# Making every fourth lo weight piece by an adding transfer in a one-core decoder trunk

## The chip, the cores and the metric

The kernel runs on one core of a Trainium2 chip. Time is device microseconds of that core. Its engines are TensorE (PE, with its weight loads as PEld), VectorE (DVE), ScalarE (ACT), GpSimd (POOL) and SyncE (SP). SP and GpSimd each issue transfers from a queue of their own; all transfers run on the core's 16 DMA engines.

## The reference

Two layers of a decoder trunk over 256 rows of width 2048, all in fp32. Layer 0 mixes by a convolution module and by differential attention, layer 1 by a gated short convolution; each layer then cross-attends into 256 memory rows and applies a squared-ReLU MLP with 8192 hidden columns:

```python
def reference(x, mem, ...):
    mem_n = rms_norm(mem, mem_norm_g)
    for l in range(DEPTH):
        hn = rms_norm(x, mix_norm_g[l])
        if l % 2 == 0:
            x = x + even_mixer(hn, ...)      # convolution module and differential attention
        else:
            x = x + odd_mixer(hn, ...)       # gated short convolution
        x = x + cross_attention(rms_norm(x, xattn_norm_g[l]), mem_n, xq_w[l], xk_w[l], xv_w[l], xo_w[l])
        x = x + sq_relu_mlp(rms_norm(x, mlp_norm_g[l]), mlp_w1[l], mlp_w2[l])
    return rms_norm(x, final_norm_g)
```

Nearly all of the work is products with weights: 1008 pieces of 128 x 1024 fp32 values, 512 KB each, every one read once.

## The kernel before, in words

A product in near-fp32 precision is made of three products in the shorter type fp32r. Weights and activations are each split into a half `hi`, the value rounded to fp32r, and a half `lo`, what the rounding lost; hi x hi, hi x lo and lo x hi are summed.

The function `weights` (L150) delivers one piece. It takes a tile `raw` and two tiles `whi` and `wlo` from rings of buffers, and gives three instructions: SP loads the piece from HBM into `raw` (L162), ScalarE copies it rounded into `whi` (L163), and VectorE writes `wlo = raw - whi` (L164). `calls` counts the pieces. The ring of `raw` has five buffers (shared with sixteen loads of the memory rows, `memraw`), those of `whi` and `wlo` three each. A buffer is taken again only when its last reader is done: `raw` when both copies of it are made, `whi` and `wlo` when TensorE's matmuls with them are.

Most products go through `wide_piece`: eight matmuls with hi weights against activations hi and lo side by side (512 columns), and eight with lo weights against the hi activations (256 columns). In the second piece of a projection one hi matmul stands behind the lo ones, so that TensorE's order is 8 hi, 8 lo, 7 hi, 8 lo, 1 hi. `proj_rows` (tiles `mmr`) and the narrow `proj` (keys, gates) use the same pieces.

Instructions run in order on each engine, and loads are issued in order by SP. Buffers decide how far the engines run ahead of TensorE, and a scheduler places the instructions of different pieces, residuals, norms and attention among one another. The token "lo" fixes the order of the subtractions among VectorE's work. Beside the weights, VectorE does residuals, the 31-tap convolution and the lo halves of activations; ScalarE does hi halves, squares, exponentials and evacuations of PSUM (`sum`, L208); GpSimd, after the start, only clears `ahl` eight times (L435) in the attention of layer 0.

Small tiles come from the pool `tmp`: `t32` (seven buffers), `rb` (three), `pexp` (four) and `diag` (two). `diag` is the diagonal matrix by which `spread` lays a norm's row values over the partitions with a matmul `nmb`.

Of the kernel before, what the change touches and what calls it, by code (L numbers as in the profile page):

```python
# [10 lines left out]
F32 = mybir.dt.float32  # L11
F32R = mybir.dt.float32r
I32 = mybir.dt.int32
AF = mybir.ActivationFunctionType
ALU = mybir.AluOpType
AX = mybir.AxisListType

P = 128
D = 2048
S = 256  # L20
# [25 lines left out]
def trunk(ctx: ExitStack, tc: tile.TileContext, d):  # L46
    nc = tc.nc
    V, A, T, G = nc.vector, nc.scalar, nc.tensor, nc.gpsimd
# [1 line left out]
    const = ctx.enter_context(tc.tile_pool(name="const", bufs=1))  # L50
    xpool = ctx.enter_context(tc.tile_pool(name="xpool", bufs=1))
    half = ctx.enter_context(tc.tile_pool(name="half", bufs=13))
    wraw = ctx.enter_context(tc.tile_pool(name="wraw", bufs=5))
    wspl = ctx.enter_context(tc.tile_pool(name="wspl", bufs=3))
    prob = ctx.enter_context(tc.tile_pool(name="prob", bufs=4))
    tmp = ctx.enter_context(tc.tile_pool(name="tmp", bufs=2))
    small = ctx.enter_context(tc.tile_pool(name="small", bufs=4))
# [4 lines left out]
    def f(ap):  # L62
        return ap.bitcast(F32)
# [23 lines left out]
    def col(name, c=0):  # L87
        i = VEC[name] + c
        return gvec[:, i:i + 1] if i < NG else vec[:, i - NG:i - NG + 1]
# [5 lines left out]
    def load_vec():  # L95
        nc.sync.dma_start(out=vec, in_=d["vec"][:, NG:])
        lv = vec[:, VEC["lam"] - NG:VEC["lam"] - NG + 256].rearrange("p (a b) -> p a b", a=4)
        lp = tmp.tile([P, S], F32, tag="t32", name="lp", bufs=7)[:, :128].rearrange("p (a b) -> p a b", a=2)
        V.tensor_tensor(lp, lv[:, 0:4:2], lv[:, 1:4:2], op=ALU.mult)
        ls = small.tile([P, 2], F32, name="ls", bufs=1)  # L100
        V.reduce_sum(out=ls, in_=lp, axis=AX.X)
        le = small.tile([P, 2], F32, name="le", bufs=1)
        A.activation(le, ls, AF.Exp)
        V.tensor_tensor(neglam, le[:, 1:2], le[:, 0:1], op=ALU.subtract)
        V.tensor_scalar(neglam, neglam, -LAM0, None, op0=ALU.add)
        V.tensor_scalar(subg, col("subln_g"), 1.0 - LAM0, None, op0=ALU.mult)
# [10 lines left out]
    rate, calls, strict = [0], [0], [False]  # L117

    def ordered(i, token):

        tc.stamp_issue_order_token(i.ins, token)
# [7 lines left out]
    def run_later(n, upto):  # L129
        while n and background and background[0][0] <= upto:  # L130
            background.pop(0)[1]()
            n -= 1

    def run_stages(upto):
        while True:
            due = [e for e in stages if e[0] <= upto]
            if not due:
                return
            stages.remove(due[0])
            due[0][1]()  # L140

    def mm(*a, **k):
        i = T.matmul(*a, **k)  # L143
        if strict[0]:
            ordered(i, "pe")
# [6 lines left out]
    def weights(src):  # L152
        run_later(rate[0], calls[0])
        run_stages(calls[0])
        calls[0] += 1
        raw = wraw.tile([P, 1024], F32, tag="raw", name="raw")
        hi = wspl.tile([P, 1024], F32R, tag="whi", name="whi")
        lo = wspl.tile([P, 1024], F32R, tag="wlo", name="wlo")
        n = 512 if calls[0] == 1 else 1024
        for i in range(0, 1024, n):  # L160
            o = slice(i, i + n)
            nc.sync.dma_start(out=raw[:, o], in_=src[:, o])  # L162
            A.copy(hi[:, o], raw[:, o])  # L163
            ordered(V.tensor_tensor(lo[:, o], raw[:, o], f(hi[:, o]), op=ALU.subtract), "lo")  # L164
        return hi, lo

    def block(ps, hi, lo, act, k, first, last):
# [16 lines left out]
    def proj_group(srcs, act, order=(0, 1), wide=True):  # L184


        pp = [ps_mm.tile([P, 512], F32, tag="mm", name="mm")[:, :(2 * S if wide else S)] for _ in srcs]
        for g in order:
            if g == order[-1] and len(srcs) > 1:
                run_stages(END)  # L190
            for src, ps in zip(srcs, pp):
                hi, lo = weights(src[:, g * 1024:(g + 1) * 1024])
                first, last = g == order[0], g == order[-1]
                if wide:
                    wide_piece(ps, hi, lo, act, g * 8, first, last)
                    continue
                for j in range(8):
                    w = slice(j * P, (j + 1) * P)
                    block(ps, hi[:, w], lo[:, w], act, g * 8 + j, first and j == 0, last and j == 7)
        return pp  # L200
# [4 lines left out]
    def summed(ps):  # L205

        t = tmp32("sum")
        A.copy(t, ps[:, S:])  # L208
        V.tensor_tensor(t, ps[:, :S], t, op=ALU.add)  # L209
        return t  # L210
# [58 lines left out]
    def spread(rows):  # L269
        ps = ps_nm.tile([P, 512], F32, tag="nm", name="nmb")[:, :S]  # L270
        for t in range(2):
            dg = tmp.tile([P, P], F32, tag="diag", name="diag")
            A.activation(dg, ident, AF.Copy, scale=rows[:, t:t + 1])
            mm(ps[:, t * P:(t + 1) * P], ones, dg, start=True, stop=True)
        return ps

    def rstd_rows(acc, n, pool=None, name="rrow"):

        v = small.tile([P, 2], F32, tag="rs_v", name="rs_v")
        V.tensor_scalar(v, mean_rows(acc, n), EPS, None, op0=ALU.add)  # L280
        return rsqrt(v, 2, pool, name)
# [12 lines left out]
        return y  # L294

    def to_sbuf(ps, pool=None, name="rb"):
        r = pool.tile([P, S], F32, tag=name, name=name) if pool else tmp.tile([P, S], F32, tag="rb", name=name, bufs=3)
        A.copy(r, ps)
        return r

    def rstd(acc, n):
        return to_sbuf(spread(rstd_rows(acc, n)))
# [13 lines left out]
            V.tensor_tensor(self.acc, self.acc, sq, op=ALU.add)  # L316

    def tmp32(name="t32"):
        return tmp.tile([P, S], F32, tag="t32", name=name, bufs=7)

    def residual(k, ps, nxt, ss, gname):

# [15 lines left out]
        return softmax_from(src, nm, width, scale)  # L338

    def softmax_from(src, bias, width, scale):  # L340
        p = tmp.tile([P, S], F32, tag="pexp", name="pexp", bufs=4)
        sm = small.tile([P, 1], F32, tag="psum", name="psum")
        A.activation(p[:, :width], src, AF.Exp, bias=bias, scale=scale, accum_out=sm)
        inv = small.tile([P, 1], F32, tag="pinv", name="pinv")
        V.reciprocal(inv, sm)
        return p, inv
# [4 lines left out]
    def even_mixer():  # L351
# [17 lines left out]
        def x_spread():  # L369
            rr["bc"] = to_sbuf(spread(rr["col"]))  # L370
# [4 lines left out]
        strict[0] = True  # L375
        pps = [proj_rows(d["even_v"][0], xa.hi, xa.lo, load_x)]
        load_vec()
        pps.append(proj_rows(d["even_v"][1], xa.hi, xa.lo))
        rc, r = rr["col"], rr["bc"]
# [19 lines left out]
        def scores(h, q, k):  # L399
            pr = {}  # L400
            banks = [ps_at.tile([P, 512], F32, tag="at", name="sc") for _ in range(2)]
            for t in range(2):
                tq = slice(t * P, (t + 1) * P)
                for c in range(2):
                    e = slice(c * 64, (c + 1) * 64)
                    ps = banks[c][:, t * S:(t + 1) * S]
                    mm(ps, q[e, 0, tq], k[e, 0], start=True, stop=False)
                    mm(ps, q[e, 1, tq], k[e, 0], start=False, stop=False)
                    mm(ps, q[e, 0, tq], k[e, 1], start=False, stop=True)
            for t in range(2):  # L410
                wd = (t + 1) * P
                for c in range(2):
                    sc = tmp32("scm")
                    mn = small.tile([P, 1], F32, tag="mx", name="mn")
                    V.tensor_tensor_reduce(
                        out=sc[:, :wd], in0=banks[c][:, t * S:t * S + wd],
                        in1=mask.rearrange("p a b -> p (a b)")[:, S - wd:],
                        scale=1.0, scalar=-NEG, op0=ALU.add, op1=ALU.min, accum_out=mn)
                    pr[t, c] = softmax_from(sc[:, :wd], mn, wd, -1.0)
            for t in range(2):  # L420
                wd = (t + 1) * P
                (p0, i0), (p1, i1) = pr[t, 0], pr[t, 1]
                V.tensor_tensor(i1, i1, neglam, op=ALU.mult)
                A.activation(p1[:, :wd], p1[:, :wd], AF.Copy, scale=i1)
                V.scalar_tensor_tensor(p0[:, :wd], p0[:, :wd], i0, p1[:, :wd], op0=ALU.mult, op1=ALU.add)
            stage(D1, lambda: turn(h, pr))
# [38 lines left out]
        def head_norm(h, orow):  # L465
            on = tmp32("on")
            V.tensor_tensor(on, orig[:, h], to_sbuf(spread(orow[:, 2 * h:2 * h + 2])), op=ALU.mult)
            rr["co"].put(h, on)
# [269 lines left out]
    r = spread(rstd_rows(ss.acc, D))  # L738
    for g in range(8):
        o = slice(2 * g, 2 * g + 2)  # L740
# [62 lines left out]
```

## Time and profile before

| what | value |
|---|---|
| median of 3 runs | 2928.85 us (2928.50 to 2928.92) |
| the profiled execution's own time | 2928.61 us |
| its span, first to last instruction | 2926.8 us |
| granted TensorE clock | 0.998 |
| TensorE busy | 2907.2 us, 99% |
| VectorE busy | 2000.0 us, 68% |
| ScalarE busy | 1456.8 us, 50% |
| GpSimd busy | 3.9 us |
| transfers | 540.12 MB; SP's queue 58.0% of 16 engines' span |

The span is the stretch that the profiler saw; the time has 1.8 us around it. A group of instructions is named by its line, engine, and the tiles it writes and reads (`wlo<-raw,whi`). Idle time of an engine that ends with "<-" was ended by the one named. TensorE's busy time covers pipelined matmuls, so 99% says that it seldom waited, not that it ran at its peak.

### The profile page before, as it was taken

The page shows a single profiled execution, that of the slowest core. Times are in us where ns is not written, and L with a number is a line of the kernel's source. Part 1 is how long each engine was busy: PE and PEld are TensorE (multiplying, and loading weights), DVE is VectorE, ACT ScalarE, POOL GpSimd, SP SyncE. Part 2 cuts the span into 40 slices and gives each one's busy share as a digit, 9 for nine tenths or more (in the row PEclk, how much of TensorE's full clock was granted, in tenths as well). Part 3 has the DMA queues.
Part 4 walks back from the last instruction along what each step waited for, and adds up shares of the span by engine and source line. Part 5 has one row for each costly group of instructions (what it writes and reads, how often), then busy time and mean ns, then how long its engine had stood idle before and what let it go on. Part 6 is the DMA issues. An engine that isn't in the chain of part 4 may idle for free.

```text
span 2926.8 us, 44172 instructions
## 1 busy us (share of the span) xinstructions
PE 2907.2 (99%) x17304; PEld 2583.8 (88%) x17304; DVE 2000.0 (68%) x3132; ACT 1456.8 (50%) x2133; POOL 3.9 (0%) x20
## 2 busy tenths in 40 slices
PE   9999999999999999999999999999999999999998
PEld 7999988898888888888888899888988888888887
DVE  7899987767666656666777764467676666566665
ACT  6665455555544535445544443455555445354453
POOL 0000000000000000000000000000000000000000
PEclk9999999999999999999999999999999999999999
DMA  7454565545565665666655655655455656656564
GB/s 249 163 191 167 180 187 188 171 151 178 184 191 187 190 187 187 189 190 190 182 192 197 202 191 187 192 189 170 142 188 183 191 188 189 189 190 188 188 188 136
DMA packets 150401, 540.12 MB, mean 185 GB/s; under 512 B 16688, under 2 KB 16816, under 8 KB 150192
## 3 DMA queue, kind: packets, MB, share of 16 engines
q1 hardware_dynamic: 150192, 537.30, 58.0%
q8 instruction: 136, 2.23, 0.3%
q14 instruction: 73, 0.60, 0.1%
HBM read 535.13 MB, written 2.10 MB: 184 GB/s over the span
## 4 chain that ended last, share of the span: by engine, by line
PE 99%; DVE 0%; DMA 0%; ACT 0%; issue 0%; DVEq 0%; SPq 0%; ACTq 0%
PE mm L143 89%; PE mmr L143 8%; PE pox L143 1%; PE sx L143 1%; PE nmb L143 0%; PE sc L143 0%; PE nmr L143 0%; PE po L143 0%; DVE x L741 0%; PE ptx L148 0%; DMA x<-xT 0%; PE ptd L148 0%; ACT xn L254 0%; DVE x L324 0%; DVEq L798 0%
## 5 line engine op out<-in xcount | busy, mean ns | idle before, releaser
L163 ACT CAST whi<-raw 128x1024 fp32r<-128x1024 f32 (+1 forms) x1009 | 1060.3, 1051 | 829.4 <-PE mm L143 702.2
L164 DVE TENSOR_TENSOR wlo<-raw,whi 128x1024 fp32r<-128x1024 f32 (+1 forms) x1009 | 1233.6, 1223 | 278.4 <-ACT whi L163 260.5
L143 PE MATMUL mm<-xn,whi 128*128 128x512 f32 (+1 forms) x4096 | 997.5, 379 | 0.0
L143 PEld LDWEIGHTS mm<-xn,whi 128*128 128x128 f32 x4096 | 724.7, 189 | 115.6
L143 PE MATMUL mm<-xn,wlo 128*128 128x256 f32 x3840 | 572.9, 282 | 0.0
L143 PEld LDWEIGHTS mm<-xn,wlo 128*128 128x128 f32 x3840 | 537.8, 190 | 34.7
L143 PE MATMUL mm<-hid,whi 128*128 128x512 f32 x2048 | 514.1, 392 | 0.0
L143 PEld LDWEIGHTS mm<-hid,whi 128*128 128x128 f32 x2048 | 368.9, 189 | 65.9
L208 ACT COPY sum<-mm 128x256 f32<-128x256 f32 x224 | 83.4, 372 | 533.0 <-PE mm L143 532.8
L324 DVE TENSOR_TENSOR x<-x,mm 128x256 f32<-128x256 f32 x384 | 161.5, 421 | 265.9 <-PE mm L143 259.2
L209 DVE TENSOR_TENSOR sum<-mm,sum 128x256 f32<-128x256 f32 x224 | 95.0, 424 | 313.2 <-ACT sum L208 312.7
L143 PEld LDWEIGHTS mm<-hid,wlo 128*128 128x128 f32 x2048 | 279.4, 190 | 19.9
L143 PE MATMUL mm<-hid,wlo 128*128 128x256 f32 x2048 | 285.6, 282 | 0.0
L143 PE MATMUL mm<-mem,whi 128*128 128x256 f32 x1024 | 185.4, 284 | 0.0
L143 PEld LDWEIGHTS mm<-mem,whi 128*128 128x128 f32 x1024 | 158.8, 190 | 0.0
L143 PE MATMUL mm<-mem,wlo 128*128 128x256 f32 x512 | 144.9, 283 | 0.0
L143 PE MATMUL mmr<-whi,mem 128*128 128x512 f32 x512 | 137.3, 390 | 0.0
L143 PE MATMUL mm<-o,whi 128*128 128x512 f32 x512 | 129.3, 393 | 0.0
L505 DVE SCALAR_TENSOR_TENSOR cv<-a,vec,cv 128x255 f32<-128x255 f32 (+14 forms) x240 | 111.5, 465 | 3.4
L143 PEld LDWEIGHTS mmr<-whi,mem 128*128 128x128 f32 x512 | 95.7, 188 | 19.5
L143 PEld LDWEIGHTS mm<-o,whi 128*128 128x128 f32 x512 | 92.2, 189 | 17.3 <-DVE o L251 0.9
L143 PEld LDWEIGHTS mm<-mem,wlo 128*128 128x128 f32 x512 | 97.4, 190 | 0.0
(165 smaller groups left out, 1803.6 us busy)
## 6 DMA issues: line engine op xcount, KB each, us to landing
raw<-w SPq DMA_DIRECT2D x512, 512.0 KB, 4.1
raw<-odd_in SPq DMA_DIRECT2D x96, 512.0 KB, 4.6
raw<-even_in SPq DMA_DIRECT2D x64, 512.0 KB, 4.4
raw<-xk SPq DMA_DIRECT2D x64, 512.0 KB, 3.7
raw<-xv SPq DMA_DIRECT2D x64, 512.0 KB, 3.5
raw<-xq SPq DMA_DIRECT2D x64, 512.0 KB, 3.9
raw<-xo SPq DMA_DIRECT2D x64, 512.0 KB, 3.8
raw<-even_out SPq DMA_DIRECT2D x32, 512.0 KB, 4.3
```

What stands on the lines that cost most here:

```text
L143: i = T.matmul(*a, **k)
L163: A.copy(hi[:, o], raw[:, o])
L164: ordered(V.tensor_tensor(lo[:, o], raw[:, o], f(hi[:, o]), op=ALU.subtract), "lo")
L208: A.copy(t, ps[:, S:])
L209: V.tensor_tensor(t, ps[:, :S], t, op=ALU.add)
L324: V.tensor_tensor(x[:, k], x[:, k], ps[:, i * S:(i + 1) * S], op=ALU.add)
L505: ordered(V.scalar_tensor_tensor(cv[:, c, s:], a[:, c, :S - s], col("conv_a_w", i + j), cv[:, c, s:], op0=ALU.mult, op1=ALU.add), "lo")
```

## The change

For calls 20, 24, 28 and so on to 1008 (248 pieces) the lo half is made in another way. ScalarE still writes `whi`. It also writes the negated, rounded value of `raw` into `wlo`, which is -hi, and a transfer from GpSimd's queue then adds `raw` to `wlo` on its way: raw - hi, as before. VectorE has no part in these pieces. To make room, the ring of `raw` goes from five buffers to four, and those of `whi` and `wlo` from three to four; `t32` goes from seven to six, `rb` from three to two, `pexp` from four to three, `diag` from two to one.

```diff
--- before.py
+++ after.py
@@ -50,8 +50,8 @@
     const = ctx.enter_context(tc.tile_pool(name="const", bufs=1))
     xpool = ctx.enter_context(tc.tile_pool(name="xpool", bufs=1))
     half = ctx.enter_context(tc.tile_pool(name="half", bufs=13))
-    wraw = ctx.enter_context(tc.tile_pool(name="wraw", bufs=5))
-    wspl = ctx.enter_context(tc.tile_pool(name="wspl", bufs=3))
+    wraw = ctx.enter_context(tc.tile_pool(name="wraw", bufs=4))
+    wspl = ctx.enter_context(tc.tile_pool(name="wspl", bufs=4))
     prob = ctx.enter_context(tc.tile_pool(name="prob", bufs=4))
     tmp = ctx.enter_context(tc.tile_pool(name="tmp", bufs=2))
     small = ctx.enter_context(tc.tile_pool(name="small", bufs=4))
@@ -95,7 +95,7 @@
     def load_vec():
         nc.sync.dma_start(out=vec, in_=d["vec"][:, NG:])
         lv = vec[:, VEC["lam"] - NG:VEC["lam"] - NG + 256].rearrange("p (a b) -> p a b", a=4)
-        lp = tmp.tile([P, S], F32, tag="t32", name="lp", bufs=7)[:, :128].rearrange("p (a b) -> p a b", a=2)
+        lp = tmp.tile([P, S], F32, tag="t32", name="lp", bufs=6)[:, :128].rearrange("p (a b) -> p a b", a=2)
         V.tensor_tensor(lp, lv[:, 0:4:2], lv[:, 1:4:2], op=ALU.mult)
         ls = small.tile([P, 2], F32, name="ls", bufs=1)
         V.reduce_sum(out=ls, in_=lp, axis=AX.X)
@@ -157,11 +157,16 @@
         hi = wspl.tile([P, 1024], F32R, tag="whi", name="whi")
         lo = wspl.tile([P, 1024], F32R, tag="wlo", name="wlo")
         n = 512 if calls[0] == 1 else 1024
+        added = calls[0] > 16 and calls[0] % 4 == 0
         for i in range(0, 1024, n):
             o = slice(i, i + n)
             nc.sync.dma_start(out=raw[:, o], in_=src[:, o])
             A.copy(hi[:, o], raw[:, o])
-            ordered(V.tensor_tensor(lo[:, o], raw[:, o], f(hi[:, o]), op=ALU.subtract), "lo")
+            if added:
+                A.activation(lo[:, o], raw[:, o], AF.Copy, scale=-1.0)
+                G.dma_start(out=lo[:, o], in_=raw[:, o], accum_op=ALU.add)
+            else:
+                ordered(V.tensor_tensor(lo[:, o], raw[:, o], f(hi[:, o]), op=ALU.subtract), "lo")
         return hi, lo
 
     def block(ps, hi, lo, act, k, first, last):
@@ -269,7 +274,7 @@
     def spread(rows):
         ps = ps_nm.tile([P, 512], F32, tag="nm", name="nmb")[:, :S]
         for t in range(2):
-            dg = tmp.tile([P, P], F32, tag="diag", name="diag")
+            dg = tmp.tile([P, P], F32, tag="diag", name="diag", bufs=1)
             A.activation(dg, ident, AF.Copy, scale=rows[:, t:t + 1])
             mm(ps[:, t * P:(t + 1) * P], ones, dg, start=True, stop=True)
         return ps
@@ -294,7 +299,7 @@
         return y
 
     def to_sbuf(ps, pool=None, name="rb"):
-        r = pool.tile([P, S], F32, tag=name, name=name) if pool else tmp.tile([P, S], F32, tag="rb", name=name, bufs=3)
+        r = pool.tile([P, S], F32, tag=name, name=name) if pool else tmp.tile([P, S], F32, tag="rb", name=name, bufs=2)
         A.copy(r, ps)
         return r
 
@@ -316,7 +321,7 @@
             V.tensor_tensor(self.acc, self.acc, sq, op=ALU.add)
 
     def tmp32(name="t32"):
-        return tmp.tile([P, S], F32, tag="t32", name=name, bufs=7)
+        return tmp.tile([P, S], F32, tag="t32", name=name, bufs=6)
 
     def residual(k, ps, nxt, ss, gname):
 
@@ -338,7 +343,7 @@
         return softmax_from(src, nm, width, scale)
 
     def softmax_from(src, bias, width, scale):
-        p = tmp.tile([P, S], F32, tag="pexp", name="pexp", bufs=4)
+        p = tmp.tile([P, S], F32, tag="pexp", name="pexp", bufs=3)
         sm = small.tile([P, 1], F32, tag="psum", name="psum")
         A.activation(p[:, :width], src, AF.Exp, bias=bias, scale=scale, accum_out=sm)
         inv = small.tile([P, 1], F32, tag="pinv", name="pinv")
```

In the changed kernel the load is L163, the hi copy L164, the negation L166, the transfer L167 and the subtraction L169.

On ScalarE, in the w2 part of layer 0's MLP, each row is an instruction and in brackets what it waits for: PE and DVE are those engines, DMAHW a load, DMASW a transfer from GpSimd's queue, Activation an earlier instruction of ScalarE. Before:

```order
L163 CAST whi<-raw 128x1024 [waits DMAHW7_49,PE_49]
L163 CAST whi<-raw 128x1024 [waits DMAHW0_49,DVE_49,PE_49]
L163 CAST whi<-raw 128x1024 [waits DMAHW1_49,DVE_49,PE_49]
L163 CAST whi<-raw 128x1024 [waits DMAHW2_49,DVE_49,PE_49]
L163 CAST whi<-raw 128x1024 [waits DMAHW3_49,DVE_49,PE_49]
```

With the change, at the same place:

```order
L164 CAST whi<-raw 128x1024 [waits DMAHW4_49,DVE_49,PE_49]
L164 CAST whi<-raw 128x1024 [waits DMAHW5_49,DVE_49,PE_49]
L166 ACTIVATE wlo<-raw 128x1024 [waits DMAHW6_49,DMASW1_49,PE_49]
L164 CAST whi<-raw 128x1024 [waits PE_49,Activation_49]
L164 CAST whi<-raw 128x1024 [waits DMAHW7_49,DVE_49,PE_49]
L164 CAST whi<-raw 128x1024 [waits DMAHW0_49,DVE_49,PE_49]
L164 CAST whi<-raw 128x1024 [waits DMAHW1_49,DVE_49,PE_49]
L166 ACTIVATE wlo<-raw 128x1024 [waits DMAHW2_49,DMASW2_49,PE_49]
```

Every fourth piece has its negation ahead of its hi copy; the negation waits for the load, for the last transfer into the same lo buffer and for TensorE's matmuls with it.

On SP, in the MLP of layer 0, the loads of weight pieces before, each behind VectorE's subtraction that frees its buffer:

```order
L162 DMA raw<-w 128x1024 [waits DMAHW7_49,DVE_49]
L162 DMA raw<-w 128x1024 [waits DMAHW0_49,DVE_49]
L162 DMA raw<-w 128x1024 [waits DMAHW1_49,DVE_49]
L162 DMA raw<-w 128x1024 [waits DMAHW2_49,DVE_49]
L162 DMA raw<-w 128x1024 [waits DMAHW3_49,DVE_49]
```

With the change:

```order
L163 DMA raw<-w 128x1024 [waits DMAHW0_49,DVE_49]
L163 DMA raw<-w 128x1024 [waits DMAHW1_49,DVE_49]
L163 DMA raw<-w 128x1024 [waits DMAHW3_49,DVE_49]
L163 DMA raw<-w 128x1024 [waits DMAHW2_49,DMASW1_49]
L163 DMA raw<-w 128x1024 [waits DMAHW4_49,DVE_49]
```

Every fourth load now waits for a GpSimd-queue transfer, since that reads the raw buffer which the load fills again.

GpSimd's own queue, in the attention of layer 0, held only the clearing of `ahl` before. With the change:

```order
L167 DMA wlo<-raw 128x1024 [waits DMAHW0_49,DMASW1_49,Activation_49]
L167 DMA wlo<-raw 128x1024 [waits DMAHW4_49,DMASW2_49,Activation_49]
L167 DMA wlo<-raw 128x1024 [waits DMAHW1_49,DMASW3_49,Activation_49]
L167 DMA wlo<-raw 128x1024 [waits DMAHW6_49,DMASW4_49,Activation_49]
L440 MEMSET ahl 128x2x128 [waits DVE_49,Pool_49] x2
L167 DMA wlo<-raw 128x1024 [waits DMAHW2_49,DMASW5_49,Activation_49]
```

The two clearings of a pair of heads stand between the transfers; 234 of the 248 transfers come behind the last of them.

## The prediction

> **What bounds the kernel now.** I read the busy times first, then TensorE's waits, then the chain of waits.
>
> ```profile
> PE 2907.2 (99%) x17304; PEld 2583.8 (88%) x17304; DVE 2000.0 (68%) x3132; ACT 1456.8 (50%) x2133; POOL 3.9 (0%) x20
> PE 99%; DVE 0%; DMA 0%; ACT 0%; issue 0%; DVEq 0%; SPq 0%; ACTq 0%
> PE mmr L143 <- ACT whi L163: 6.1, 1, 6.1
> PE nmb L143 <- ACT diag L273: 2.9, 1, 2.9
> PE nmr L143 <- DVE accsq L316: 1.9, 1, 1.9
> ```
>
> TensorE is busy 2907.2 of 2926.8 us and the chain that ended last is 99% TensorE. Its waits are 6.1 us for the first weights and two of 2.9 and 1.9 us around norms: 10.9 us in all, none for a lo half. So VectorE's 68% and ScalarE's 50% set nothing, and the change can only matter if it makes a piece's lo half late. The question is how much time a piece has. The timeline of the w2 part of layer 0's MLP gives it:
>
> ```profile
> 1203.64 1.23 DVE L164 TENSOR_TENSOR wlo<-raw,whi 128x1024 fp32r<-128x1024 f32 x1 [0.61 <-ACT whi L163]
> 1204.89 0.33 SPq L162 DMA_DIRECT2D raw<-w  x1
> 1205.75 1.92 PEld L143 LDWEIGHTS mm<-hid,whi 128*128 128x128 f32 x9
> 1206.30 1.05 ACT L163 CAST whi<-raw 128x1024 fp32r<-128x1024 f32 x1 [2.70 <-PE mm L143]
> 1207.38 1.22 DVE L164 TENSOR_TENSOR wlo<-raw,whi 128x1024 fp32r<-128x1024 f32 x1 [0.20 <-ACT whi L163]
> 1207.71 1.13 PEld L143 LDWEIGHTS mm<-hid,wlo 128*128 128x128 f32 x8
> 1208.77 1.47 PEld L143 LDWEIGHTS mm<-hid,whi 128*128 128x128 f32 x7
> 1210.28 1.13 PEld L143 LDWEIGHTS mm<-hid,wlo 128*128 128x128 f32 x8
> 1211.34 1.92 PEld L143 LDWEIGHTS mm<-hid,whi 128*128 128x128 f32 x9
> ```
>
> Two pieces take 1211.34 - 1205.75 = 5.59 us, so four take 11.2. A subtraction that ended at 1203.64 + 1.23 = 1204.87 let SP issue the next load at 1204.89: a handoff of 0.02 to 0.03 us. ScalarE's end at 1207.35 let VectorE start at 1207.38, about 0.03 us too. The pieces of each stage, counted by VectorE's subtractions (each row: busy us and count, clock, DMA share, GB/s):
>
> ```profile
> 353.00:408.00 55.00, 25.38 (x21) 1.00 0.67 197
> 440.00:536.00 96.00, 41.81 (x35) 1.00 0.58 189
> 536.00:659.00 123.00, 42.85 (x35) 1.00 0.47 155
> 744.00:1455.00 711.00, 311.61 (x255) 1.00 0.61 188
> 1461.00:1813.00 352.00, 152.75 (x125) 1.00 0.58 194
> 1814.00:1900.00 86.00, 39.20 (x32) 1.00 0.65 195
> 2204.00:2911.00 707.00, 307.58 (x252) 1.00 0.60 184
> ```
>
> Four pieces take 10.5, 11.0, 14.1, 11.15, 11.26, 10.75 and 11.22 us in these rows. The third is cross attention, which has other matmuls between the pieces.
>
> **The change part by part.** 248 pieces change (calls 20, 24, ... 1008). VectorE loses 248 subtractions and ScalarE gains 248 negations:
>
> ```profile
> L163 ACT CAST whi<-raw 128x1024 fp32r<-128x1024 f32 (+1 forms) x1009 | 1060.3, 1051 | 829.4 <-PE mm L143 702.2
> L164 DVE TENSOR_TENSOR wlo<-raw,whi 128x1024 fp32r<-128x1024 f32 (+1 forms) x1009 | 1233.6, 1223 | 278.4 <-ACT whi L163 260.5
> L273 ACT ACTIVATE diag<-ident,rrow 128x128 f32<-128x128 f32 x30 | 10.4, 396 | 8.1 <-DVE rrow L293 8.1
> ```
>
> VectorE gives back 248 x 1.223 = 303 us, ScalarE takes on 248 x 1.05 = 260 us and comes to about 59%. Neither is on the chain, so both are worth nothing directly. The fewer buffers for small tiles and the single diag buffer touch work that feeds norms; that is covered by the three pieces made ahead, and where it isn't (the final norm has no matmuls to hide behind) a second diag (0.40 us) and its matmul cost under 1 us. The fourth hi/lo slot and the lost raw slot leave eight pieces in the pipeline as before. GpSimd's clearing of ahl now stands in one queue with the transfers, but it waits for buffers that a head group earlier released; I take 0, and at worst one period at each of three places, some 35 us.
>
> What counts is the new **loop through one slot**. The changed pieces are every fourth, and both rings have four slots, so in the dense stages all changed pieces share one raw and one lo slot. SP may issue load n only when transfer n-4 has landed; ScalarE negates when the load is there; the GpSimd-queue transfer follows; then the loop begins again. All in one line, nothing of it overlaps itself. If its length exceeds the time TensorE takes for four pieces, it sets the pace. It holds SP's and ScalarE's queues too: behind the waiting load stand the three next loads, behind the negation that waits for it the next four hi casts, so no other piece can run on past it by more than the slots hold. Its terms:
>
> ```profile
> q1 hardware_dynamic: 150192, 537.30, 58.0%
> raw<-w SPq DMA_DIRECT2D x512, 512.0 KB, 4.1
> DMA to landing us min/median/max: 3.4/4.0/7.8
> L435 POOL MEMSET ahl<- 128x256 f32 x8 | 2.4, 312 | 197.4 <-DVE pinv L423 159.3 <-PE po L143 38.1
> ```
>
> Load: 4.1 us median (3.4 at best). Negation: 1.05. Three handoffs: 0.1. Transfer: the trace has no accumulating transfer and none from GpSimd's queue, so it is bounded. It can't be much shorter than the quickest load of its size, 3.4. An add must fetch two tiles where a load fetches one; the DMA engines' own time for a load is 58.0% of 2926.8 = 1698 us over 537.30 MB / 0.524 = 1025 loads, 1.66 us, so a slow case is the slowest load plus that, 7.8 + 1.66 = 9.5. I take the median load in this traffic plus one more reading, 4.1 + 1.66, plus 0.6 for issue by GpSimd: twice its longest row, the 0.31 us memset, with 0 and 1.22 (one subtraction of VectorE in its way) as bounds. That is 6.4, and the loop 4.1 + 1.05 + 0.1 + 6.4 = 11.65 us, 0.5 more than the 11.15 of the largest stage.
>
> The Trainium skill would have it shorter. "DMA: Bandwidth & Descriptors" (Anatomy of one DMA, the gpsimd path) fits such a transfer by about 2.0 us plus bytes over 436 GB/s, and "Collectives: The Full Stack" (The bandwidth ceiling) says an add by DMA needs two source reads and so runs at half the rate: an estimate of 2.0 + 2.4 = 4.4 us, a loop of 9.7, and nothing lost. No run here shows it, and the same fit without the add gives 3.2, below the shortest load of this trace, 3.4, in a quiet system.
>
> Sum, excess of 11.65 over each row's four pieces, times the fours: 353:408 1.15 x 5 = 6; 440:536 0.65 x 9 = 6; 744:1455 0.50 x 64 = 32; 1461:1813 0.39 x 31 = 12; 1814:1900 0.90 x 8 = 7; 2204:2911 0.43 x 63 = 27; the dense stretches between, some 300 us, 27 x 0.5 = 13. Cross attention's 14.1 and the even layer's interleaved stage hide it. Together 103 us. The profiled execution has a span of 2926.8 and a time of 2928.61, against a median of 2928.85; 2928.85 + 103 is **3032 us, 3.5% slower**.
>
> **The rivals.** *Hidden:* the transfer takes under 11.15 - 5.25 = 5.9 us, or the loads land at 3.4 and it may take 6.6. Then the loop is shorter than TensorE's four pieces, the lo half is ready before its matmul (it has 11.2 - 1.1 = 10.1 us after the slot's last use, of which the transfer and negation need 7), and the time stays 2928.85 within 4 us. For it: the quickest loads, the deeper hi/lo ring, and the skill's estimate above; against it: the engines are already 58 to 67% busy, so loads and transfers stretch one another.
>
> *The DMA engines are the bound:* four loads and a double-length transfer need 6 x 1.66 = 10 of 11.15 us, no bound yet. If adding runs slower than fetching, say at the time of four loads, they need 8 x 1.66 = 13.3 us and set the pace: 2.1 us x 64 + 2.0 x 31 + 2.5 x 8 + 2.1 x 63 + 2.8 x 5 + 2.3 x 9 + 2.1 x 27 = 440 us, or 3370. Nothing in the trace speaks for a slow add but that none is there. Up to 9.5 for the transfer, a loop of 14.75, it would be some 750 us.
>
> *Faster:* VectorE's relief and the third piece ahead remove the waits of 2.9 and 1.9 us at the norms. That is all there is, since the 6.1 at the start comes before the first changed piece: 2924, 0.16%. Against it: even that is less than can be told apart.
>
> *A locked-out GpSimd:* "SBUF — State Buffer" (Who interferes with whom) says that GpSimd cannot write a transfer's descriptors while VectorE runs an operation that uses both its ports, but that a tensor_tensor with two inputs is no such operation. By that rule the subtractions do not delay the issue and the loop loses only the 0.6 for it; were it otherwise, 1.22 for each would add some 250 us more. Its chance is small.
>
> **How the numbers follow.** The loop somewhat over four pieces: 0.40. Hidden: 0.38. The DMA engines or a locked-out GpSimd, far over: 0.17. Faster: 0.05, of which part stays within 0.2%. A measurement of this kernel tells about 0.2%, 5.9 us, from no change. So slower 0.57, same 0.39, faster 0.04. The likeliest case alone runs from 2940 to 3200 (a loop up to 0.8 us longer than taken); the range takes in the hidden case below and most of the DMA-bound case above: 2925 to 3400.
>
> **What would show it.** Right: TensorE shows waits for lo at the every-fourth pieces in the MLPs, about 0.5 us each, SP waits for the transfer, the transfer lands some 6.4 us after its negation, the four-piece period is about 11.6 and the waits are gone in cross attention. Hidden: no TensorE wait for lo, a transfer below 5.9. DMA-bound: a DMA share near 0.95 with loads well over 4.1. The sum is wrong above all if the transfer's landing is off: each 0.1 us of it is 20 us of time once the loop decides, and nothing before.

## The result and the profile after

The changed kernel takes 2974.64 us (median of 4, 2972.40 to 2976.55) against 2928.68 for the kernel before beside it: a ratio of 1.0156, 95% interval 1.0144 to 1.0169. It is 46 us slower; 103 were forecast. The profiled execution has a span of 2974.8 us, 48.0 longer than the profiled one of before; it is the longest of the four, 1.9 us over their median. From its page (busy times, the chain that ended last, transfers by queue, issues to landing) and TensorE's waits:

```profile
PE 2918.6 (98%) x17304; PEld 2586.0 (87%) x17304; DVE 1711.3 (58%) x2884; ACT 1674.1 (56%) x2381; POOL 214.8 (7%) x268
PE 88%; DMA 5%; DVE 3%; ACT 2%; issue 1%; SPq 0%; ACTq 0%; DVEq 0%
q1 hardware_dynamic: 150192, 537.30, 54.7%
q0 software_dynamic: 35712, 130.04, 23.2%
raw<-w SPq DMA_DIRECT2D x512, 512.0 KB, 4.5
wlo<-raw POOLq DMA_DIRECT2D x248, 512.0 KB, 5.1
L167 POOL DMA_DIRECT2D wlo<-raw x248 | 211.1, 851 | 2733.9 <-ACT wlo L166 1420.5
PE nmb L143 <- ACT diag L278: 16.4, 14, 2.9
PE ptd L148 <- DVE pexp L430: 6.9, 4, 1.9
PE sx L143 <- DVE xq L706: 5.7, 8, 0.9
PE mm L143 <- DMA wlo<-raw: 4.9, 6, 1.6
784.00:1494.00 710.00, 710.00 (x4070) 624.64 (x4069) 373.42 (x540) 398.56 (x542) 54.45 (x64) 1.00 0.83 236
```

VectorE is down 289 us of the 303 costed, and ScalarE is up 217 of 260. The chain that ended last was 99% TensorE before; now 88% of it is TensorE and 5% loads and transfers. A transfer lands in 5.1 us, not 6.4, and the last row (us, then each engine's busy time, clock, DMA share) shows layer 0's MLP with 64 transfers in it and TensorE busy for all of its 710 us. TensorE waits for a lo half for only 4.9 us in the whole execution. Its larger waits are at `nmb` for the diagonal matrix (14 waits, where before there was one of 2.9 us) and, where before there was none, at `ptd` for the softmax buffers and at `sx` for the query halves.

Where the 46 us arose is read from stretches of matmuls that are the same work in both. Rows of the chain of waits (start, us, what), first before and then after:

```profile
314.45 37.43 PE mm L143 x312
744.40 710.93 PE mm L143 x4074
1813.68 87.07 PE mmr L143 x384
2203.92 707.68 PE mm L143 x4056
```

```profile
344.84 37.43 PE mm L143 x312
784.34 709.53 PE mm L143 x4064
1854.97 87.07 PE mmr L143 x384
2252.27 706.28 PE mm L143 x4046
```

By the first pair the kernel is 30.4 us late (all in layer 0's mixing and head norms). The rows of the two MLPs begin ten matmuls later in the changed kernel, so there the ends are compared (start plus length): it is 38.5 us late at the end of the first MLP (8.1 more, from layer 0's values, output projection and cross attention), 41.3 by the third pair (the odd layer added 2.8) and 47.0 at the end of the last MLP (the second cross attention and what stands around it added 5.7); the last 1.0 falls behind the MLP, at the final norm. The MLPs, where the forecast put 59 of its 103 us, cost nothing: from the first to the last matmul with `hid` (the MLP's hidden values), layer 0's takes 625.5 us in both kernels (826.2 to 1451.7 and 864.7 to 1490.2).

### The profile page after: what moved, and what is told of

Its sections match the earlier page's. It is cut to its first block, busy times and chain, and to the rows that moved or that the text cites. A ratio compares the mean times of both kernels' runs of the same rounds, so it can differ in the third digit from the quotient of the medians.

```text
span 2974.8 us, 44444 instructions
## 1 busy us (share of the span) xinstructions
PE 2918.6 (98%) x17304; PEld 2586.0 (87%) x17304; DVE 1711.3 (58%) x2884; ACT 1674.1 (56%) x2381; POOL 214.8 (7%) x268
## 3 DMA queue, kind: packets, MB, share of 16 engines
q0 software_dynamic: 35712, 130.04, 23.2%
## 4 chain that ended last, share of the span: by engine, by line
PE 88%; DMA 5%; DVE 3%; ACT 2%; issue 1%; SPq 0%; ACTq 0%; DVEq 0%
PE mm L143 79%; PE mmr L143 7%; DMA wlo<-raw 2%; ACT whi L164 1%; DVE wlo L169 1%; DMA raw<-even_out 1%; DMA raw<-even_in 1%; PE pox L143 1%; DVE cv L510 1%; PE sx L143 1%; ACT wlo L166 0%; DMA raw<-xq 0%; PE nmb L143 0%; DMA raw<-odd_in 0%; DMA raw<-even_v 0%
## 5 line engine op out<-in xcount | busy, mean ns | idle before, releaser
L164 ACT CAST whi<-raw 128x1024 fp32r<-128x1024 f32 (+1 forms) x1009 | 1045.8, 1047 | 501.1 <-PE mm L143 344.6
L169 DVE TENSOR_TENSOR wlo<-raw,whi 128x1024 fp32r<-128x1024 f32 (+1 forms) x761 | 930.7, 1223 | 476.3 <-ACT whi L164 465.2
L166 ACT ACTIVATE wlo<-raw 128x1024 fp32r<-128x1024 f32 x248 | 263.0, 1060 | 471.8 <-PE mm L143 377.4
L167 POOL DMA_DIRECT2D wlo<-raw x248 | 211.1, 851 | 2733.9 <-ACT wlo L166 1420.5
```

Source lines behind the costliest of these rows:

```text
L166: A.activation(lo[:, o], raw[:, o], AF.Copy, scale=-1.0)
L167: G.dma_start(out=lo[:, o], in_=raw[:, o], accum_op=ALU.add)
```

## The experiments

Each was timed in three rounds beside the kernel before. The question was how the 46 us divide among the cut small buffers, ScalarE's negation and the transfers, and when the loop through a slot decides.

### The pools alone

```diff
-        added = calls[0] > 16 and calls[0] % 4 == 0
+        added = False
```

> The changed pools alone, every lo half by VectorE as before. If the cut of the small buffers (diag, pexp, rb, t32) makes the loss: 2955 to 2975 us, with TensorE still waiting at nmb for diag (about 16 us in all) and at ptd for pexp (about 7 us). If the transfers make it (DMA traffic, late lo halves, ScalarE's extra work): 2929 within 4 us, since the deeper hi/lo ring costs nothing. In between, the two share it.

Measured: 2950.64 us, ratio 1.0075 (1.0060 to 1.0090). So 22 of the 46 us come with no transfer at all. The two buffer cuts that show in TensorE's waits were then made alone in the kernel before:

```diff
-            dg = tmp.tile([P, P], F32, tag="diag", name="diag")
+            dg = tmp.tile([P, P], F32, tag="diag", name="diag", bufs=1)
```

> The kernel before with one diag buffer in place of two, nothing else. With the changed pools alone TensorE waited 15.9 us at nmb for diag against 2.9 before, and the eight head norms came every 7.55 us against 6.19 (8 x 1.36 = 10.9). If the single diag buffer is that: 2941 to 2946 us. If it needs the other cuts too: under 2934.

```diff
-        p = tmp.tile([P, S], F32, tag="pexp", name="pexp", bufs=4)
+        p = tmp.tile([P, S], F32, tag="pexp", name="pexp", bufs=3)
```

> The kernel before with three pexp buffers in place of four, nothing else. A head's softmax makes four, so the fourth exponential waits until the first two are merged. If that holds TensorE at ptd as in the changed pools (4.3 us of waits there, and knock-on): 2933 to 2938 us. If the loss in the even layer has another cause: 2929 within 2.

One diag buffer: 2947.34 us, ratio 1.0061 (1.0044 to 1.0078), 18.5 us, slightly more than expected. Three pexp buffers: 2931.53 us, ratio 1.0009 (1.0000 to 1.0019), 2.7 us, under the 4 to 9 expected and at the edge of what can be told. Together 21.2 of the 22. The chain of waits of the kernel with one diag buffer (pieces of 0.04 us and less are left out) shows how writing that matrix, 0.40 us, stops TensorE for 1.4:

```profile
282.93 0.85 PE mm L143 x7
283.80 1.04 ACT whi L163
284.85 0.31 ACT diag L273
285.20 0.49 PE nmb L143 x2
285.69 5.64 PE mm L143 x47
291.36 1.04 ACT whi L163
```

A norm's row values are laid out by two matmuls, each with its own diagonal matrix. With one buffer the second matrix can be written only after the first matmul. TensorE's work is the cover I counted on, but ScalarE at that moment has a 1.04 us hi cast in hand, released by the same matmuls; the 0.40 us matrix stands behind it, and the second `nmb` stands next in TensorE's own order. TensorE waits for both, from 283.78 to 285.20. Before, the chain of the same place goes from matmul to matmul:

```profile
283.04 0.44 PE nmb L143 x4
283.48 5.75 PE mm L143 x48
289.23 0.44 PE nmb L143 x4
```

The head norms follow one another at 291.36 - 283.80 = 7.56 us with one buffer and 289.23 - 283.04 = 6.19 us with two: 1.37 us each, eight times, 11 of the 18.5.

### Negations without transfers

```diff
             if added:
                 A.activation(lo[:, o], raw[:, o], AF.Copy, scale=-1.0)
-                G.dma_start(out=lo[:, o], in_=raw[:, o], accum_op=ALU.add)
-            else:
+            if True:
                 ordered(V.tensor_tensor(lo[:, o], raw[:, o], f(hi[:, o]), op=ALU.subtract), "lo")
```

> The changed kernel with ScalarE's negation at every fourth piece, but no transfer: VectorE then writes lo over it as for the other pieces. It keeps ScalarE's extra 260 us and its place in the order and takes away the DMA traffic and the loop. If the negation ahead of evacuations makes the transfers' part of the loss: 2965 to 2975. If the transfers themselves make it: 2951 within 4, as the changed pools alone.

Measured: 2957.99 us, ratio 1.0099 (1.0084 to 1.0114): 7.3 above the pools alone, between the two expectations, so both theories had a part. TensorE now has these waits, which it has not with the pools alone:

```profile
PE sx L143 <- DVE xq L705: 7.0, 8, 0.9
```

They are the eight heads of the two cross attentions. Two successive heads of layer 0's, with the pools alone and then with the negations:

```profile
581.28 5.59 PE mm L143 x32
609.83 5.59 PE mm L143 x32
```

```profile
581.17 5.59 PE mm L143 x32
610.85 5.59 PE mm L143 x32
```

A head takes 28.55 and 29.68 us. The changed kernel's timeline shows what stands in line there:

```profile
618.35 1.06 ACT L166 ACTIVATE wlo<-raw 128x1024 fp32r<-128x1024 f32 x1 [2.42 <-PE mm L143]
619.32 0.35 ACT L213 COPY sum<-mm 128x256 f32<-128x256 f32 x1
619.56 2.00 ACT L164 CAST whi<-raw 128x1024 fp32r<-128x1024 f32 x2
621.46 0.40 ACT L705 CAST xq<-sum 128x256 fp32r<-128x256 f32 x1
621.59 1.23 DVE L169 TENSOR_TENSOR wlo<-raw,whi 128x1024 fp32r<-128x1024 f32 x1 [1.01 <-ACT whi L164]
622.74 0.42 DVE L706 TENSOR_TENSOR xq<-sum,xq 128x256 fp32r<-128x256 f32 x1
623.21 1.93 PE L143 MATMUL sx<-hl,xq 128*128 128x256 f32 x14 [0.68 <-DVE xq L706]
```

The negation waits for TensorE's lo matmuls of four pieces ago, just when TensorE also finishes a projection whose result ScalarE must evacuate. The 1.06 us go ahead of the evacuation; two hi casts follow, and behind them the query's hi half on ScalarE and, behind the subtraction that the second cast releases, its lo half on VectorE. The scores wait for the end of that chain. This stage was taken to hide everything because its pieces are far apart; they are, but what waits there is a chain through ScalarE, not a lo half. ScalarE is idle four tenths of the time and it made no difference.

### The transfer without its add

```diff
-                G.dma_start(out=lo[:, o], in_=raw[:, o], accum_op=ALU.add)
+                G.dma_start(out=lo[:, o], in_=raw[:, o], accum_op=ALU.bypass)
```

> The changed kernel with the add left out of the transfer: it copies raw over lo (with the rounding), so the lo halves of these pieces are wrong. If the second operand sets the transfer's length: DMA engine time from 2.8 us to 1.6 to 1.9 each, landing from 5.1 to about 4.2 us, and the time falls to 2962 to 2970. If GpSimd's issue (0.85 us) and the rounding set it: landing stays at 4.8 to 5.1 and the time at 2972 to 2977.

Measured: 2960.63 us, ratio 1.0108 (1.0091 to 1.0125), a little below the first case. From its page, GpSimd's groups, and the landing of its transfers and then of its loads (min, median, max):

```profile
q0 software_dynamic: 35712, 130.04, 12.1%
L167 POOL DMA_DIRECT2D wlo<-raw x248 | 131.6, 531 | 2797.8 <-ACT wlo L166 1460.2 <-ACT sum L213 1168.6 <-PE mm L143 55.7
DMA to landing us min/median/max: 2.8/3.5/6.7
DMA to landing us min/median/max: 3.4/4.3/8.8
```

The copy lands in 3.5 us and takes the engines 12.1% x 2959.5 / 248 = 1.44 us; the add lands in 5.1 and takes 23.2% x 2974.8 / 248 = 2.78. So the add costs 1.6 us of landing, near the 1.66 taken, and 1.9 times the engines' time. Of the 1.6, 0.32 is GpSimd's longer issue (0.85 against 0.53). By the Trainium skill, "Collectives: The Full Stack" (The bandwidth ceiling), an add by DMA reads two sources and so runs at half the rate; this pair agrees. The Trainium skill's fit in "DMA: Bandwidth & Descriptors" (Anatomy of one DMA, the gpsimd path) had given an estimate of 3.2 us for the copy and 4.4 for the add; 3.5 and 5.1 were measured in this traffic, which is nearer than the 4.7 and 6.4 that I worked out from loads. A copy is 2.6 us dearer than the negations alone (where VectorE still made every subtraction), the add another 14.0.

In this order the 46 us divide into one diag buffer 18.5, pexp 2.7, the rest of the pools 0.8, the negations on ScalarE 7.3, plain transfers 2.6 and the add 14.0. That they add up is no evidence: each step is the difference of two neighbouring kernels, and the 0.8 is what is left of the pools. In another order the parts can differ by some microseconds, as the diag buffer does below.

### Where the transfers cost

```diff
-        added = calls[0] > 16 and calls[0] % 4 == 0
+        added = calls[0] > 80 and calls[0] % 4 == 0
```

> The changed kernel with no transfers in the first 80 pieces (the even layer's mixing, where VectorE runs the convolution). If transfers and loads crowd one another there, the 18 us lost between 54 and 259 us go: 2955 to 2960 us. If the cut buffers alone lose them: 2970 to 2976, as the changed kernel.

Measured: 2964.65 us, ratio 1.0127 (1.0111 to 1.0144), between the two cases. Sixteen changed pieces (negation and transfer) in the even layer's mixing are worth 10 us, not 18. The rest there is buffers: the row of 312 matmuls that starts at 314.45 before and at 344.84 in the changed kernel starts at 333.57 here and at 334.32 with the pools alone. The loads of this layer's weights (`even_in`) between 54 and 314 us land in 4.6 us in the changed kernel and in 4.1 in this one.

```diff
-        added = calls[0] > 16 and calls[0] % 4 == 0
+        added = calls[0] % 4 == 0 and (240 < calls[0] <= 496 or calls[0] > 752)
```

> The changed kernel with transfers only in the two MLPs (128 of the 248). My corrected theory, that a transfer is free wherever the loop through its slot (4.5 + 1.06 + 5.1 + 0.1 = 10.8 us) stays under four pieces and nothing latency-bound stands behind the negation on ScalarE: 2951 within 3, the time of the changed pools alone. Rival, that every transfer costs the same: 128/248 of the 24 us between that and the changed kernel on top, 2963.

Measured: 2950.66 us, ratio 1.0074 (1.0059 to 1.0089): the time of the pools alone to 0.02 us. The 128 transfers in the MLPs are free, so the 24 us between the pools alone and the changed kernel come from the other 120. With two diag buffers again (five t32 for the room), those 128 and then all 248 transfers:

```diff
-            dg = tmp.tile([P, P], F32, tag="diag", name="diag", bufs=1)
+            dg = tmp.tile([P, P], F32, tag="diag", name="diag")
...
-        return tmp.tile([P, S], F32, tag="t32", name=name, bufs=6)
+        return tmp.tile([P, S], F32, tag="t32", name=name, bufs=5)
```

> Transfers in the MLPs alone and two diag buffers again; the room comes from t32 (five in place of six), pexp stays at three. If the diag buffer and the place of the transfers make the loss: 2931 to 2934 us (pexp's 2.7 is left). If five t32 buffers are too few, or the deeper hi/lo ring costs something of its own: 2940 or more. No theory has it under 2927, since TensorE has no wait to give back.

> The changed kernel with two diag buffers (t32 five). With the single buffer's 18.5 us gone: 2955 to 2958. If diag waits and transfers hide in one another: 2960 to 2970.

Measured: 2933.83 us, ratio 1.0017 (1.0008 to 1.0027), and 2958.65 us, ratio 1.0100 (1.0085 to 1.0115). The second is 0.65 us over its first case. The diag buffer accounts for 16 to 17 us in both, with one t32 buffer less. No version was under 2928.68; behind the start, TensorE's waits at norms, 4.8 us, were all there was to give back.

### When the loop decides

The small buffers were put back in two other ways: with all pools as before, and with three hi slots beside four lo and four raw slots. Of each the lines of the rings are shown; the cuts of t32, rb, pexp and diag are undone as well.

```diff
-    wraw = ctx.enter_context(tc.tile_pool(name="wraw", bufs=4))
-    wspl = ctx.enter_context(tc.tile_pool(name="wspl", bufs=4))
+    wraw = ctx.enter_context(tc.tile_pool(name="wraw", bufs=5))
+    wspl = ctx.enter_context(tc.tile_pool(name="wspl", bufs=3))
```

> The transfers with all pools as before the change (raw 5, hi and lo 3, small tiles uncut). Buffer theory: under 2945 us, no wait of TensorE for diag or pexp. Transfer theory: 2960 us or more. With three lo slots a piece has 2 pieces and 7 hi matmuls, some 7.3 us, from its slot's last use; negation and transfer need 1.06 + 5.1 + 0.1 = 6.3, so TensorE waits for the transfer only where it takes over 6 us.

```diff
-        hi = wspl.tile([P, 1024], F32R, tag="whi", name="whi")
+        hi = wspl.tile([P, 1024], F32R, tag="whi", name="whi", bufs=3)
```

> The change with the small buffers as before; room is made by three hi slots in place of four (lo keeps four, raw four). Buffer theory: 2929 to 2940 us and the waits for diag and pexp gone. Transfer theory: 2965 to 2975, as the changed kernel. The loop through one slot is the same 10.8 us as in the changed kernel, under four pieces, so the MLPs run at TensorE's pace in both theories.

Measured: 3014.02 us, ratio 1.0294 (1.0279 to 1.0310), and 3035.91 us, ratio 1.0371 (1.0336 to 1.0406). The buffer theory is refuted by both: without the buffer loss the kernel is slower still. The transfer theory had 2960 or more for the first, which holds, and 2965 to 2975 for the second, which does not. TensorE's wait for the transfer is now its largest; the first row is of the kernel with old pools, the next of that with three hi slots:

```profile
PE mm L143 <- DMA wlo<-raw: 45.3, 51, 3.7
```

```profile
PE mm L143 <- DMA wlo<-raw: 59.6, 71, 2.7
800.00:1500.00 700.00, 51.78 (x61) 1.00 0.78 231
```

With three hi slots, 700 us of layer 0's MLP hold 61 transfers, one in some 11.4 to 11.5 us, where TensorE needs 11.15 for four pieces: the loop sets the pace. One round of it, and below it one of the changed kernel in the same MLP:

```profile
1003.84 1.06 ACT L166 ACTIVATE wlo<-raw 128x1024 fp32r<-128x1024 f32 x1 [0.65 <-DMA raw<-w]
1005.20 0.85 POOL L167 DMA_DIRECT2D wlo<-raw  x1 [11.07 <-ACT hid L249]
1010.82 0.33 SPq L163 DMA_DIRECT2D raw<-w  x1
1015.23 1.06 ACT L166 ACTIVATE wlo<-raw 128x1024 fp32r<-128x1024 f32 x1 [0.86 <-DMA raw<-w]
```

```profile
1009.97 1.06 ACT L166 ACTIVATE wlo<-raw 128x1024 fp32r<-128x1024 f32 x1 [2.22 <-PE mm L143]
1011.32 0.86 POOL L167 DMA_DIRECT2D wlo<-raw  x1 [10.33 <-ACT sum L213]
```

With three hi slots the negation waits for its load, and the round is 1.36 (negation and handoff) + 5.62 (transfer) + 4.41 (load) = 11.39 us. In the changed kernel the negation waits for TensorE, so the loop has time to spare, but little: 1.35 + 5.1 + 4.5 by its medians is 10.95, and TensorE's four pieces are 11.15. The fourth hi slot, for which the small buffers were cut, goes with transfers that stay hidden in the MLPs: from the first to the last matmul with `hid`, layer 0's MLP takes 636.3 us with three hi slots, 631.0 with the old pools, and 625.5 with four. These are 11 and 6 us of losses of 107 and 85; with 18 and 8 in the other MLP, most of both losses lies outside the MLPs, and where was not followed. Why loads and transfers of the kernel with three hi slots are longer (4.9 and 6.0 us by the medians of its page, against 4.5 and 5.1) is not settled: the DMA share in that stretch, 0.78, is lower than the changed kernel's 0.83. That they come in bursts once the loop holds SP back is a guess that no run here isolates.

Last, every second piece by transfer:

```diff
-        added = calls[0] > 16 and calls[0] % 4 == 0
+        added = calls[0] > 16 and calls[0] % 2 == 0
```

> The changed kernel with every second piece by transfer. The loop through a slot is as long as before, but the DMA engines need 4 x 1.59 for the loads and 2 x 2.78 for the transfers, 11.9 us of the 11.15 that TensorE takes for four pieces. If the engines' time adds up so, they set the pace: 3130 us or more, DMA share near 1. If loads and transfers share the engines at no loss and only the loop counts: under 3000.

Measured: 3210.09 us, ratio 1.0962 (1.0946 to 1.0978). The stretch from 900 to 1000 us of it (busy us of each engine, clock, DMA share, GB/s):

```profile
900.00:1000.00 100.00, 98.06 (x556) 84.75 (x556) 37.91 (x58) 58.36 (x69) 14.46 (x17) 1.00 1.01 274
```

The DMA engines are full there. From the first to the last matmul with `hid`, this MLP takes 664.1 us, 6% more than 625.5, at a DMA share of 0.98; the engines' time expected, 11.9 us where TensorE takes 11.15, would make it 7%. The rival of engines as the bound is real in the MLPs; the change stops short of it, at 0.83. But the two MLPs make 68 of the 281 us lost. The rest is not shown to be the engines: loads land in 5.6 us and transfers in 6.5, so the loop through a slot was longer too, and not as long as before.

## Why the prediction was wrong

**The sign was right, its main reason was not.** That the time fell on the slower side, inside 2925 to 3400, is luck: what made it slower stood in the sum at nothing. The loop through one slot, "11.65 us, 0.5 more than the 11.15", was to give all 103 us. In the changed kernel it is 10.95 in the MLPs and gives nothing there. The step that failed is the transfer's length: 6.4 taken, 5.1 measured. The second operand was sized well (1.66 against 1.6, of which 0.32 is the longer issue), and the issue is inside the 5.1 (0.85 us on GpSimd). What was too long is the base: a load under traffic, 4.1, plus 0.6 for the issue, where a plain transfer of this queue lands in 3.5. The loads, 4.5 in place of 4.1, and the handoffs, 0.3 in place of 0.1, went the other way. The rival "hidden" described the MLPs, by a margin of 0.2 us, and the prediction's own rule said that each 0.1 us is worth 20 us or nothing around that point; I still summed one value instead of giving the edge its weight.

**The loop exists**, but decides elsewhere and in other kernels: with three hi slots it runs at some 11.4 us, and in layer 0's output projection of the changed kernel it appears in the chain of waits:

```profile
505.89 3.80 DMA raw<-even_out
509.80 1.07 ACT wlo L166
511.15 5.69 DMA wlo<-raw
516.89 5.62 DMA raw<-even_out
```

Load, negation, transfer and the next load follow one another (pieces of 0.28 us and less are left out), and the round takes 516.89 - 505.89 = 11.0 us; four pieces took 10.97 in this stage before. The chain then leaves the loop by a hi cast, a subtraction and a residual, so what the loop costs there is not isolated.

**"That is covered by the three pieces made ahead"** was the most costly step: the smaller buffers were put at under 1 us and cost 22. The pieces ahead cover a late weight. They don't cover an instruction that TensorE's own order has put next, and the second `nmb` was such a one at each of the eight head norms. A wait of one `nmb` had been priced at under 1 us at the final norm alone.

**"Cross attention's 14.1 and the even layer's interleaved stage hide it"** was wrong for the same reason. A loop of 11.65 is indeed hidden in a stage of 14.1 us per four pieces, but the negation also lengthens a chain through ScalarE there (7.3 us, 7.0 by TensorE's waits at `sx`), and in the even layer 16 changed pieces cost 10 us, with loads that land half a microsecond later. By which wait they cost them is not isolated.

**Right:** the number of instructions and their durations, VectorE's total within 14 us (ScalarE's was put 43 too high), the ring lengths for weights (with the other small buffers they cost 0.8 us), GpSimd's `ahl` costing nothing visible, and the DMA engines not being the bound at every fourth piece. A GpSimd locked out by VectorE is not seen either: the 248 issues take 0.84 to 1.00 us each, so none holds a subtraction of 1.22. The faster case did not come: the waits of 2.9 and 1.9 us at the norms stayed in every kernel.

## What to carry to other kernels

When a change pays for a new buffer with small ones, price the small ones first: ask of each whether a matmul stands next in TensorE's order that needs two of them, since nothing made ahead covers that. An engine's idle share does not say that another microsecond on it is free; look for the chain in which it evacuates a result that TensorE waits for. And where a forecast rests on a loop within a few per cent of the pace that hides it, the two outcomes are to be given as two cases, because the sum between them is a time that neither has.

## What the runs showed that was not expected

An adding transfer of 512 KB within SBUF lands in 5.1 us and a plain one in 3.5, shorter than the 4.3 us of the loads of the same size beside it, though it is issued by GpSimd in 0.5 to 0.9 us. And a single buffer of 128 x 128 values, written 36 times in the kernel, was worth 18.5 us of 2929 without ScalarE or TensorE having an instruction more to do.
